# Turned copies of the first two heads' k, made behind the split of their tile

## The chip, the cores and the metric

The kernel runs on one core of one Trainium2 chip. The core has four compute engines that run beside each other, each through its own list of instructions in order: TensorE (PE: matmuls; PEld is its weight load), VectorE (DVE), ScalarE (ACT) and GpSimd (POOL). SyncE (SP) only issues transfers, and POOL and ACT issue some too. An instruction that waits holds up everything behind it in its engine's list. The metric is device time in microseconds, the median of several runs; lower is better.

## The reference, cut to what matters

A two-layer decoder trunk over 512 tokens of width 1024, all in float32. Each layer has two attention branches of 8 heads of 64, then a gated merge, an output projection and a feed-forward part (dense in layer 0, eight experts with top-2 routing in layer 1):

```python
for l in range(DEPTH):
    h = rmsnorm(x, g_mix[l]); p = h @ w_in[l]
    q_sb, k_sb, v_sb, q_fx, k_fx, v_fx, f_pre, gate_pre = jnp.split(p, splits, axis=-1)
    y_sb = merge_heads(stick_breaking_attention(q_sb, k_sb, v_sb)) @ w_o_sb[l]
    qf, kf = rmsnorm(split_heads(q_fx), g_q[l]), rmsnorm(split_heads(k_fx), g_k[l])
    y_fx = merge_heads(forgetting_attention(qf, kf, v_fx, log_f)) @ w_o_fox[l]
    x = x + (g_sb * y_sb + g_fx * y_fx) @ w_out[l]
    x = x + ffn(rmsnorm(x, g_ffn[l]))
```

In both branches a block of 128 queries meets all keys up to its end. The forgetting branch ("fox") adds a decay to each score and takes a softmax; the stick-breaking branch ("sb") turns each score into log-probabilities, sums them from the right and takes an exponential.

## The kernel before, in words

**Precision.** A float32 operand is kept as two fp32r tiles, a rounded high part and the rest, the low part. A product takes three matmuls (high by high, high by low, low by high): L320, L321, L322 in the projections.

**q and k.** The tile of two heads is split by `qk_split` into one tile for each head: the head's high part lies in its own 64 partitions, the low part in the other 64 (ACT, L524 or L526; DVE, L532 or L534). One matmul of 128 partitions then gives high by high plus low by low. The cross terms need k with its halves exchanged, the "turned" copy: `turn` makes it with two transfers of 64 partitions, issued by POOL (L542). So a score is two matmuls (L677 in fox, L768 in sb): q by k, and q by the turned k. The score of a block is complete only when the second is done.

**Fox rounds.** `fox_rounds` has 32 rounds, 8 heads by 4 query blocks, the longest block (512 keys) first. A round issues: the scores of one block into one of four PSUM tiles "pa"; the transposes (L617) of the weights from three rounds before; their split (ACT L631, DVE L633); once a head is complete, the products with v (L589, L590); the sum of score and decay with its minimum (DVE L688, tile `s` from `pa` and `cb`), the exponential (ACT L693) and the division (DVE L699, L700). The decay tile `cb` has two buffers; it is fetched by POOL (L655) and masked by POOL (L665), block by block, each mask behind the minimum of the block before.

**Weave.** PE is kept busy by a filler: between the rounds of fox stand the projections for sb's q, k and v ("mm" tiles, two of them); between the rounds of sb stand the gates and an output projection.

**What sets the order.** ACT's list stands as the program was traced. The lists of PE, DVE, POOL and SP are laid out by a scheduler at build time: it takes the instruction that its own model has ready first, and of those that are ready the one that was traced first. So where a line stands in the program decides where its instructions, and those that need their results, stand in the lists. Tiles named `b` come from one pool of 59 buffers.

**The lines in question.** `mixer` runs the fox projections (`qk_tiles`, with `qk_norm` behind each tile), then weaves `fox_rounds`, and later `sb_rounds`. In both, the turned copy of head 0 is traced when the rounds begin and that of head h+1 in the first round of head h:

```python
self.turned = {}
self.turn(k, 0)
...
if u % NT == 0:
    self.turn(k, h + 1)
```

Of the kernel before, what the change touches and what calls it, by code (L numbers as in the profile page):

```python
# [26 lines left out]
H = 8  # L27
# [45 lines left out]
def f32v(t):  # L73
    return t.bitcast(F32)


class Trunk:
# [434 lines left out]
    def qk_dst(self, a, lst):  # L512

        t = [self.blk() for _ in range(2)]
        lst.append(t)
        return t

    def qk_split(self, src, sc, *dst):
        nc = self.nc
        for h in range(2):  # L520
            s, o = slice(h * DH, h * DH + DH), slice(DH - h * DH, P - h * DH)
            t = dst[h]
            if sc == 1.0:
                nc.scalar.copy(t[s], src[s])  # L524
            else:
                nc.scalar.activation(t[s], src[s], AF.Copy, scale=sc)  # L526
        for h in range(2):
            s, o = slice(h * DH, h * DH + DH), slice(DH - h * DH, P - h * DH)
            t = dst[h]
            lo = t[o]  # L530
            if sc == 1.0:
                nc.vector.tensor_sub(lo, src[s], f32v(t)[s])  # L532
            else:
                nc.vector.scalar_tensor_tensor(lo, src[s], sc, f32v(t)[s], op0=ALU.mult, op1=ALU.subtract)  # L534

    def turn(self, k, h):

        if h < H:
            t = k[h // 2][h % 2]
            r = self.blk()  # L540
            for s, o in ((slice(0, DH), slice(DH, P)), (slice(DH, P), slice(0, DH))):
                self.nc.gpsimd.dma_start(f32v(r)[o], f32v(t)[s])  # L542
            self.turned[h] = r

    def qk_of(self, q, k, h):

        qs = q[h // 2][h % 2]
        return (qs, k[h // 2][h % 2]), (qs, self.turned[h])

    def vproj(self, hh, hl, v, rc=None, pre=None):  # L550

# [94 lines left out]
    def fox_rounds(self, q, k, v, cum, ys):  # L646
        nc = self.nc
        N = H * NT
        st = {}
        cbs = {}  # L650

        def bc(h):
            if h < H:
                cbs[h] = self.ap.tile([P, S], F32, tag="cb", bufs=2, name=self.nm("cb"))
                nc.gpsimd.dma_start(cbs[h], cum[h:h + 1].to_broadcast([P, S]))  # L655
                if CM:
                    mask(h, NT - 1)

        def idx(u):
            h, r = divmod(u, NT)  # L660
            return h, NT - 1 - r if CM else r

        def mask(h, qb):
            c = cbs[h][:, qb * P:qb * P + P]
            nc.gpsimd.affine_select(out=c, in_=c, pattern=[[-1, P]], compare_op=ALU.is_ge, fill=-NEG, base=0,  # L665
                                    channel_multiplier=1)

        def scores(u):
            h, qb = idx(u)
            if u % NT == 0:  # L670
                bc(h + 1)
                self.turn(k, h + 1)
            L = (qb + 1) * P
            qs = slice(qb * P, L)
            z = self.psa()
            for j, (a, b) in enumerate(self.qk_of(q, k, h)):
                nc.tensor.matmul(z[:, :L], a[:, qs], b[:, :L], start=j == 0, stop=bool(CM) and j == 1)  # L677
            if not CM:
                nc.tensor.matmul(z[:, qs], self.identb, self.fxmask, start=False, stop=True)
            st[u] = [z]  # L680

        def softmax_a(u):
            h, qb = idx(u)
            L = (qb + 1) * P
            z = st[u][0]
            s = self.ap.tile([P, S], F32, tag="s", bufs=NS, name=self.nm("s"))
            mn = self.sp.tile([P, 1], F32, tag="mn", name=self.nm("mn"))
            nc.vector.tensor_tensor_reduce(s[:, :L], z[:, :L], cbs[h][:, :L], 1.0, 1e38, op0=ALU.add,  # L688
                                           op1=ALU.min, accum_out=mn)
            if qb and CM:  # L690
                mask(h, qb - 1)
            sm = self.sp.tile([P, 1], F32, tag="sm", name=self.nm("sm"))
            nc.scalar.activation(s[:, :L], s[:, :L], AF.Exp, bias=mn, scale=-1.0, accum_out=sm)  # L693
            st[u] = [s, sm]

        def softmax_b(u):
            L = (idx(u)[1] + 1) * P
            s, sm = st[u]
            nc.vector.reciprocal(sm, sm)  # L699
            nc.vector.tensor_scalar_mul(s[:, :L], s[:, :L], sm)  # L700

        transposes, p_evac, av = self.attn_back(v, st, idx)
        self.turned = {}
        self.turn(k, 0)
        bc(0)
        yy = {}
        for r in range(N + FD + 3):
            if r < N:
                scores(r)
            if OB_ == 0 and r < N:  # L710
                softmax_a(r)
            if 0 <= r - SM < N and SM:
                softmax_b(r - SM)
            if OB_ == 1 and r < N:
                softmax_a(r)
            u = r - FD
            if 0 <= u < N:
                transposes(u)
            u -= 2
            if u % NT == NT - 1 and 0 <= u < N:  # L720
                yy[u // NT] = av(u // NT)
            u += 2
            if 0 <= u < N:
                p_evac(u)
            if OB_ == 2 and r < N:
                softmax_a(r)
            if r < N and not SM:
                softmax_b(r)
            u -= 3
            if u >= 0 and u % NT == NT - 1:  # L730
                self.y_evac(u // NT, yy.pop(u // NT), ys)
            yield
# [13 lines left out]
    def sb_rounds(self, q, k, v, ys):  # L746
        nc = self.nc
        N = H * NT
        st = {}
        yy = {}  # L750

        def idx(u):
            return divmod(u, NT)

        transposes, p_evac, av = self.attn_back(v, st, idx)

        self.turned = {}
        self.turn(k, 0)

        def scores(u):  # L760
            h, qb = idx(u)
            if u % NT == 0:
                self.turn(k, h + 1)
            L = (qb + 1) * P
            qs = slice(qb * P, L)
            z = self.psa()
            for j, (a, b) in enumerate(self.qk_of(q, k, h)):
                nc.tensor.matmul(z[:, :L], a[:, qs], b[:, :L], start=j == 0, stop=False)  # L768
            nc.tensor.matmul(z[:, qs], self.identb, self.sbmask, start=False, stop=True)
            st[u] = z  # L770

        def softplus(u):
            L = (idx(u)[1] + 1) * P
            z = st[u]
            a = self.ap.tile([P, S], F32, tag="sa", bufs=2, name=self.nm("sa"))[:, :L]
            nc.scalar.activation(a, z[:, :L], AF.Abs)
            nc.scalar.activation(a, a, AF.Exp, scale=-1.0)
            nc.scalar.activation(a, a, AF.Ln, bias=self.one)
            st[u] = z, a

        def logs(u):

            L = (idx(u)[1] + 1) * P
            z, a = st[u]
            s = self.ap.tile([P, S], F32, tag="s", bufs=NS, name=self.nm("s"))
            nc.vector.scalar_tensor_tensor(s[:, :L], z[:, :L], 0.0, a, op0=ALU.max, op1=ALU.add)
            nc.vector.tensor_tensor_scan(s[:, :L][:, ::-1], self.ones[:, :L], s[:, :L][:, ::-1], 0.0, op0=ALU.mult,
                                         op1=ALU.add)
            nc.vector.tensor_sub(s[:, :L], z[:, :L], s[:, :L])
            st[u] = [s]  # L790

        def weights(u):
            L = (idx(u)[1] + 1) * P
            s = st[u][0]
            nc.scalar.activation(s[:, :L], s[:, :L], AF.Exp)

        for r in range(N + SD + 3):
            if r < N:
                scores(r)
            u = r - SD  # L800
            if 0 <= u < N:
                transposes(u)
            u -= 2
            if u % NT == NT - 1 and 0 <= u < N:
                yy[u // NT] = av(u // NT)
            u += 2
            if r < N:
                softplus(r)
            if 0 <= r - SW < N and SW:
                weights(r - SW)  # L810
            if 0 <= u < N:
                p_evac(u)
            if r < N:
                logs(r)
            if r < N and not SW:
                weights(r)
            u -= 3
            if u >= 0 and u % NT == NT - 1:
                self.y_evac(u // NT, yy.pop(u // NT), ys)
            yield  # L820
# [1064 lines left out]
```

## Time and profile before

| | |
|---|---|
| median of 3 runs | 1715.91 us (1715.15 to 1716.56) |
| the profiled execution: its time, its span | 1717.1 us, 1715.3 us |
| busy share of the span: PE, PEld, DVE, ACT, POOL | 96%, 84%, 64%, 57%, 12% |
| mean granted clock of PE | 0.985 |
| scores of fox (L677), layer 0 and layer 1 (us from the span's start) | 95 to about 187, 862 to 952 |
| scores of sb (L768), layer 0 and layer 1 | 205 to about 325, 970 to 1090 |
| expert stage | from about 1205 |

The profile numbers are of one execution. The busy share is an average over stages with different limits, so what a change in one stage is worth is read in a window of that stage. In a timeline row the time in brackets is how long the engine was idle before the row, and the name behind the arrow is what ended that idle time.

### The profile page before, as it was taken

The page shows a single profiled execution, that of the slowest core. Times are in us where ns is not written, and L with a number is a line of the kernel's source. Part 1 is how long each engine was busy: PE and PEld are TensorE (multiplying, and loading weights), DVE is VectorE, ACT ScalarE, POOL GpSimd, SP SyncE. Part 2 cuts the span into 40 slices and gives each one's busy share as a digit, 9 for nine tenths or more (in the row PEclk, how much of TensorE's full clock was granted, in tenths as well). Part 3 has the DMA queues.
Part 4 walks back from the last instruction along what each step waited for, and adds up shares of the span by engine and source line. Part 5 has one row for each costly group of instructions (what it writes and reads, how often), then busy time and mean ns, then how long its engine had stood idle before and what let it go on. Part 6 is the DMA issues. An engine that isn't in the chain of part 4 may idle for free. (4 is left out here: it accounts for less than half of the span.)

```text
span 1715.3 us, 26180 instructions
## 1 busy us (share of the span) xinstructions
PE 1644.6 (96%) x9031; PEld 1433.5 (84%) x9031; DVE 1094.1 (64%) x1844; ACT 978.3 (57%) x1750; POOL 206.4 (12%) x315
## 2 busy tenths in 40 slices
PE   6989999999999999999989999999899999999996
PEld 6867987788888888888868987887789999999996
DVE  5578678765533332336578678655667888767984
ACT  5666589754422222324667589643656776656773
POOL 6112100002000000000122000101012202102200
PEclk9999999999999999999999999999799999999998
DMA  6333333235333332443433333352959999869993
GB/s 179 108 86 101 80 98 80 76 103 177 99 99 96 95 94 91 134 130 99 111 83 103 93 86 80 102 186 100 309 190 302 299 363 353 300 211 342 313 345 87
DMA packets 270840, 273.73 MB, mean 160 GB/s; under 512 B 11424, under 2 KB 259232, under 8 KB 270688
## 3 DMA queue, kind: packets, MB, share of 16 engines
q1 hardware_dynamic: 255936, 230.98, 42.7%
q0 software_dynamic: 12288, 37.40, 8.0%
q10 hardware_dynamic: 2464, 3.41, 0.6%
q8 instruction: 85, 1.39, 0.3%
q14 instruction: 67, 0.55, 0.1%
HBM read 250.21 MB, written 13.14 MB: 154 GB/s over the span
## 5 line engine op out<-in xcount | busy, mean ns | idle before, releaser
L320 PE MATMUL mm<-b,whi 128*128 128x512 f32 x1072 | 426.4, 398 | 4.1 <-DVE b L534 3.3
L322 PE MATMUL mm<-b,wlo 128*128 128x512 f32 x1072 | 419.5, 391 | 0.0
L321 PE MATMUL mm<-b,whi 128*128 128x512 f32 x1072 | 419.1, 391 | 0.0
L297 DVE TENSOR_TENSOR wlo<-wr,whi 128x1024 fp32r<-128x1024 f32 (+1 forms) x176 | 213.1, 1213 | 208.3 <-ACT whi L296 206.3
L296 ACT CAST whi<-wr 128x1024 fp32r<-128x1024 f32 (+1 forms) x176 | 182.9, 1042 | 262.9 <-issue 120.5
L1469 DVE TENSOR_TENSOR elo<-er,ehi 128x1408 fp32r<-128x1408 f32 (+3 forms) x200 | 305.1, 1568 | 26.0 <-ACT ehi L1468 15.5
L1468 ACT CAST ehi<-er 128x1408 fp32r<-128x1408 f32 (+3 forms) x200 | 256.1, 1324 | 22.3 <-DVE oh L1274 5.5
L320 PEld LDWEIGHTS mm<-b,whi 128*128 128x128 f32 x1072 | 201.8, 188 | 45.2 <-DVE b L534 4.6
L322 PEld LDWEIGHTS mm<-b,wlo 128*128 128x128 f32 x1072 | 201.3, 188 | 42.6 <-DVE wlo L297 0.4
L321 PEld LDWEIGHTS mm<-b,whi 128*128 128x128 f32 x1072 | 201.8, 188 | 39.1 <-issue 0.2
L356 PE MATMUL mm<-whi,b 128*128 128x256 f32 x320 | 92.3, 289 | 1.7 <-DVE b L532 1.1
L357 PE MATMUL mm<-wlo,b 128*128 128x256 f32 x320 | 91.3, 285 | 0.4 <-DVE wlo L297 0.4
L358 PE MATMUL mm<-whi,b 128*128 128x256 f32 x320 | 91.0, 285 | 0.0
L1682 PE MATMUL pa<-elo,ah 128*128 128x352 f32 (+1 forms) x264 | 85.8, 325 | 2.7 <-PEq L1621 0.3
L1683 PE MATMUL pa<-ehi,al 128*128 128x352 f32 (+1 forms) x264 | 84.7, 321 | 3.3 <-DVE al L1582 3.3
L1681 PE MATMUL pa<-ehi,ah 128*128 128x352 f32 (+1 forms) x264 | 86.5, 328 | 0.9 <-PEq L1689 0.2
L1647 PE MATMUL pa<-ehi,xh 128*128 128x352 f32 x256 | 85.8, 335 | 0.0
L1648 PE MATMUL pa<-elo,xh 128*128 128x352 f32 x256 | 83.7, 327 | 2.0 <-PEq L1621 0.5
L1648 PE MATMUL pa<-ehi,xl 128*128 128x352 f32 x256 | 83.1, 325 | 0.9 <-PEq L1621 0.3
L1647 PE MATMUL pa<-elo,xh 128*128 128x352 f32 x256 | 83.1, 325 | 0.3 <-DVE elo L1469 0.3
L1647 PE MATMUL pa<-ehi,xl 128*128 128x352 f32 x256 | 83.2, 325 | 0.0
L1648 PE MATMUL pa<-ehi,xh 128*128 128x352 f32 x256 | 83.1, 325 | 0.0
(351 smaller groups left out, 3107.6 us busy)
## 6 DMA issues: line engine op xcount, KB each, us to landing
er<-in_w_gu_exp_dram SPq DMA_DIRECT2D x248, 352.0 KB, 6.5
wr<-in_w_in_dram SPq DMA_DIRECT2D x80, 512.0 KB, 3.9
wr<-in_w_gu_dense_dram SPq DMA_DIRECT2D x44, 512.0 KB, 3.8
er<-in_w_dn_exp_dram SPq DMA_DIRECT2D x32, 704.0 KB, 10.6
wr<-in_w_dn_dense_dram SPq DMA_DIRECT2D x20, 512.0 KB, 3.4
er<-in_w_dn_exp_dram SPq DMA_DIRECT2D x16, 640.0 KB, 9.0
er<-in_w_dn_exp_dram SPq DMA_DIRECT2D x16, 528.0 KB, 10.2
b<-b POOLq DMA_DIRECT2D x64, 128.0 KB, 2.8
```

The source lines that it names most:

```text
L296: self.nc.scalar.copy(hi, raw)
L297: self.nc.vector.tensor_sub(lo, raw, f32v(hi))
L320: self.nc.tensor.matmul(ps, hi[:, j], hh[j], start=st, stop=False)
L321: self.nc.tensor.matmul(ps, hi[:, j], hl[j], start=False, stop=False)
L322: self.nc.tensor.matmul(ps, lo[:, j], hh[j], start=False, stop=sp)
L356: nc.tensor.matmul(o, a, hi[:, j], start=first, stop=False, skip_group_check=True)
L357: nc.tensor.matmul(o, a, lo[:, j], start=False, stop=False, skip_group_check=True)
L358: nc.tensor.matmul(o, b, hi[:, j], start=False, stop=last, skip_group_check=True)
L1468: self.nc.scalar.copy(hi, raw)
L1469: self.last_dve = self.nc.vector.tensor_sub(lo, raw, f32v(hi))
L1647: nc.tensor.matmul(pg, x[:, k], w[:, 0, kk], start=s0, stop=s1)
L1648: nc.tensor.matmul(pu, x[:, k], w[:, 1, kk], start=s0, stop=s1)
```

## The change

`qk_dst` now hands `qk_split` the list of k tiles as a third element when the tile is one of k. `qk_split` makes the turned copies of both heads of the first k tile at once, behind its own split. The copies are kept in the list of the tile itself, and `turn` skips a head that has its copy. The call at the start of the rounds is gone in both branches; heads 2 to 7 are traced where they were. The number and shape of all instructions stay the same.

```diff
         t = [self.blk() for _ in range(2)]
         lst.append(t)
-        return t
+        return t + [lst] * a
...
+        if len(dst) == 3 and dst[2][0][0] is dst[0]:
+            for h in range(2):
+                self.turn(dst[2], h)
 
     def turn(self, k, h):
 
-        if h < H:
+        if h < H and len(k[h // 2]) < 3 + h % 2:
...
-            self.turned[h] = r
+            k[h // 2].append(r)
...
-        return (qs, k[h // 2][h % 2]), (qs, self.turned[h])
+        return (qs, k[h // 2][h % 2]), (qs, k[h // 2][2 + h % 2])
...
-        self.turned = {}
-        self.turn(k, 0)
         bc(0)
```

The lists of ACT and SP keep their order. Those of PE, DVE and POOL change at the start of the fox rounds and at the start of the sb rounds, in both layers alike. Line numbers behind `qk_split` are 3 higher in the changed kernel (L677 is L680).

On PE, layer 0, this is where the scores of head 0 get their second matmul before: `b_1089` is the turned copy of head 0's k, `pa_1105` to `pa_1163` the scores of its four blocks, `mm_1243` the second tile of the filler, `s_1108` the weights of the first block.

```order
L320 MATMUL mm_1243<-b_131,whi_1010 128x512
L321 MATMUL mm_1243<-b_139,whi_1010 128x512
L677 MATMUL pa_1105<-b_1089,b_707 128x512
L677 MATMUL pa_1118<-b_1089,b_707 128x384
L677 MATMUL pa_1150<-b_1089,b_707 128x256
L677 MATMUL pa_1163<-b_1089,b_707 128x128
L322 MATMUL mm_1243<-b_131,wlo_1011 128x512
L320 MATMUL mm_1243<-b_132,whi_1010 128x512
L321 MATMUL mm_1243<-b_140,whi_1010 128x512
```

And now, 47 rows earlier in the list (`b_904` is the turned copy, `py_1065` the norm of the last but one tile of k, `mm_1137` the first tile of the filler):

```order
L502 MATMUL py_1065<-t_1043,mean_h 128x512
L680 MATMUL pa_1105<-b_802,b_707 128x512
L680 MATMUL pa_1105<-b_904,b_707 128x512
L503 MATMUL py_1065<-t_1044,mean_h 128x512
L680 MATMUL pa_1118<-b_802,b_707 128x384
L680 MATMUL pa_1118<-b_904,b_707 128x384
L320 MATMUL mm_1137<-b_126,whi_965 128x512
```

The scores of the first two blocks are complete before the filler begins, those of the other two in the middle of its first tile. The 17 matmuls of the second filler tile that are no longer ahead of the first transposes now stand between the transposes and the scores of head 1.

On DVE, layer 0, the end of the norms and splits of k and the first minima of fox, before:

```order
L507 SCALAR_TENSOR_TENSOR t_1065<-pa_963,g_k_201,t_1062 128x512
L312 TENSOR_TENSOR t_1070<-t_1067,t_1069 128x512
L532 TENSOR_TENSOR b_1006<-t_1065,b_1006 64x512
L532 TENSOR_TENSOR b_1007<-t_1065,b_1007 64x512
L507 SCALAR_TENSOR_TENSOR t_1083<-pa_1014,g_k_201,t_1080 128x512
L532 TENSOR_TENSOR b_1057<-t_1083,b_1057 64x512
L532 TENSOR_TENSOR b_1058<-t_1083,b_1058 64x512
L688 ISA s_1108,mn_1109<-pa_1105,cb_1092 128x512
```

And now:

```order
L691 ISA s_1108,mn_1109<-pa_1105,cb_1095 128x512
L691 ISA mn_1109 128x1
L507 SCALAR_TENSOR_TENSOR t_1071<-pa_969,g_k_201,t_1068 128x512
L691 ISA s_1121,mn_1122<-pa_1118,cb_1095 128x384
L691 ISA mn_1122 128x1
L312 TENSOR_TENSOR t_1076<-t_1073,t_1075 128x512
L532 TENSOR_TENSOR b_1012<-t_1071,b_1012 64x512
L532 TENSOR_TENSOR b_1013<-t_1071,b_1013 64x512
L691 ISA s_1153,mn_1154<-pa_1150,cb_1095 128x256
L691 ISA mn_1154 128x1
L507 SCALAR_TENSOR_TENSOR t_1089<-pa_1020,g_k_201,t_1086 128x512
L691 ISA s_1185,mn_1186<-pa_1163,cb_1095 128x128
```

All four minima of head 0 have moved between the norms and splits of the last two k tiles.

On POOL, layer 0, the middle of fox before, where `cb_1506` is the decay of head 4 and `b_1511` its turned copy:

```order
L542 DMA b_1511<-b_1006 64x512 x2
L655 DMA cb_1506<-cum_667 128x512
L665 AFFINE_SELECT cb_1359<-cb_1359 128x128
L665 AFFINE_SELECT cb_1506<-cb_1506 128x128
L665 AFFINE_SELECT cb_1359<-cb_1359 128x128 x2
```

And now (`b_1550` and `b_1553` are the turned copies of sb's heads 0 and 1):

```order
L545 DMA b_1511<-b_1012 64x512 x2
L658 DMA cb_1506<-cum_667 128x512
L668 AFFINE_SELECT cb_1359<-cb_1359 128x128
L545 DMA b_1550<-b_1485 64x512
L668 AFFINE_SELECT cb_1506<-cb_1506 128x128
L545 DMA b_1553<-b_1486 64x512
L545 DMA b_1550<-b_1485 64x512
L545 DMA b_1553<-b_1486 64x512
L668 AFFINE_SELECT cb_1359<-cb_1359 128x128 x2
```

The four copies of sb's first two heads stood behind the last mask of fox and now stand between the masks of heads 3 and 4. The copies of fox's heads 0 and 1 have kept their place in POOL's list, behind the first two masks.

## Rows read from the trace of the kernel before

**Rows 1.** The page: busy time, share of the span and instructions of each engine.
```profile
PE 1644.6 (96%) x9031; PEld 1433.5 (84%) x9031; DVE 1094.1 (64%) x1844; ACT 978.3 (57%) x1750; POOL 206.4 (12%) x315
```

**Rows 2.** Busy time in windows: length, engines, clock, DMA share, GB/s.
```profile
105.00:107.00 2.00, 2.00 (x12) 1.71 (x11) 0.68 (x2) 0.00 (x0) 0.00 (x0) 1.00 0.00 0
113.00:115.00 2.00, 0.80 (x3) 0.43 (x3) 0.49 (x2) 1.48 (x3) 0.32 (x2) 1.00 0.96 254
115.00:117.00 2.00, 0.78 (x3) 0.59 (x4) 1.71 (x7) 1.62 (x7) 0.64 (x3) 0.74 0.53 127
117.00:123.70 6.70, 6.61 (x24) 5.56 (x25) 6.64 (x23) 4.22 (x14) 2.17 (x3) 0.57 0.51 139
95.00:123.70 28.70, 23.62 (x101) 18.21 (x100) 21.39 (x65) 18.40 (x49) 5.61 (x12) 0.88 0.28 70
862.10:890.80 28.70, 23.87 (x106) 18.10 (x105) 21.41 (x64) 18.38 (x49) 5.59 (x12) 0.88 0.27 70
```

**Rows 3.** Timeline of PE, start of fox, layer 0: start, length, instruction, idle before.
```profile
94.68 0.57 PE L677 MATMUL pa<-b,b 128*128 128x512 f32 x2
105.78 0.74 PE L677 MATMUL pa<-b,b 128*128 128x512 f32 x4
112.18 0.41 PE L617 MATMUL pa<-ident,s 128*128 128x128 f32 x2 [1.69 <-DVE sm L699]
115.87 0.63 PE L677 MATMUL pa<-b,b 128*128 128x128 f32 x2 [2.00 <-DVE mn L688]
130.92 0.50 PE L320 MATMUL mm<-b,whi 128*128 128x512 f32 x1 [0.65 <-DVE b L534]
```

**Rows 4.** Timeline of POOL, fox, layer 0.
```profile
77.31 0.55 POOL L542 DMA_DIRECT2D b<-b  x1 [15.89 <-ACT b L524]
78.95 1.03 POOL L542 DMA_DIRECT2D b<-b  x2 [0.19 <-issue]
110.04 0.56 POOL L655 DMA_DIRECT2D cb<-cum  x1 [0.72 <-DVE mn L688]
114.69 0.53 POOL L665 TENSOR_SCALAR_AFFINE_SELECT cb<-cb 128x128 f32<-128x128 f32 x2 [3.04 <-DMA cb<-cum]
136.13 0.45 POOL L665 TENSOR_SCALAR_AFFINE_SELECT cb<-cb 128x128 f32<-128x128 f32 x1 [2.42 <-DMA cb<-cum]
139.24 0.29 POOL L665 TENSOR_SCALAR_AFFINE_SELECT cb<-cb 128x128 f32<-128x128 f32 x1 [2.66 <-DVE mn L688]
```

**Rows 5.** Timeline of DVE, layer 0; the last row is layer 1.
```profile
102.34 1.40 DVE L532 TENSOR_TENSOR b<-t,b 64x512 fp32r<-64x512 f32 x2 [0.69 <-ACT b L524]
106.32 0.69 DVE L688 CUSTOM_DVE_ANT_0 s<-pa,cb 128x512 f32<-128x512 f32 x1 [2.58 <-issue]
107.41 0.56 DVE L688 CUSTOM_DVE_ANT_0 s<-pa,cb 128x384 f32<-128x384 f32 x1 [0.40 <-POOL cb L665]
115.25 0.56 DVE L688 CUSTOM_DVE_ANT_0 s<-pa,cb 128x384 f32<-128x384 f32 x1 [1.76 <-POOL cb L665]
119.47 1.39 DVE L534 SCALAR_TENSOR_TENSOR b<-mm,b 64x512 fp32r<-64x512 f32 x2
136.74 1.39 DVE L532 TENSOR_TENSOR b<-mm,b 64x512 fp32r<-64x512 f32 x2 [0.31 <-ACT b L524]
882.38 0.56 DVE L688 CUSTOM_DVE_ANT_0 s<-pa,cb 128x384 f32<-128x384 f32 x1 [1.72 <-POOL cb L665]
```

**Rows 6.** Timeline of ACT, layer 0.
```profile
101.68 1.26 ACT L524 CAST b<-t 64x512 fp32r<-64x512 f32 x2 [0.82 <-DVE t L507]
107.05 0.72 ACT L693 ACTIVATE s<-s,mn 128x512 f32<-128x512 f32 x1 [4.10 <-DVE mn L688]
```

**Rows 7.** Windows at the start of sb, layer 0, columns as in rows 2.
```profile
200.00:220.00 20.00, 20.00 (x114) 17.28 (x113) 9.07 (x17) 9.40 (x21) 0.90 (x2) 1.00 0.40 104
```

**Rows 8.** The line of the turned copies: count, issue times, time to landing.
```profile
L542 POOL DMA_DIRECT2D b<-b x64: 522/524/545, 77.3 to 1051.4; - x64
DMA to landing us min/median/max: 2.2/2.8/6.4
```

More of the change, by code (lines that the diff above doesn't have):

```diff
@@ L755, in sb_rounds @@
         transposes, p_evac, av = self.attn_back(v, st, idx)
-        self.turned = {}
-        self.turn(k, 0)
         def scores(u):
```

## The prediction

> **What bounds the kernel now.** I read the page's busy times first: PE is busy 96% of the span [rows 1], so a gain must come out of the 70 us in which it stands, or out of stretches at half clock. Next came windows along the first attention rounds, since the change touches only their beginning. The reader should see that PE stands in one place: from 95.0 to 123.7 in layer 0 it is busy 23.62 of 28.70 us, so it idles 5.08, and in the same stretch of layer 1 it idles 28.70 - 23.87 = 4.83 [rows 2]. At 113 to 117 it works about 40% of the time, and the granted clock then falls to a mean of 0.57, near the lower level of 1.2 GHz, for 117.0 to 123.7 [rows 2]. Third, the timelines say why. PE multiplies head 0 by k at 94.68 but by the turned k only at 105.78 [rows 3], because filler stands between in its list. DVE ends the last split of k at 103.74, idles 2.58 us and takes the first minimum at 106.32 [rows 5]. ACT, idle for 4.10 us, takes the first exponential at 107.05 [rows 6]. The copies were not late: POOL issues the first at 77.31, as soon as ACT has split the tile, the last two from 78.95 on [rows 4], and the longest landing of all 64 is 6.4 us [rows 8], so they are there by 86.4. What waits is only the order of the lists.
>
> At the start of sb nothing waits: PE is busy 20.00 of 20 us from 200 to 220 at full clock [rows 7].
>
> **The change, part by part.** No instruction is added or removed. I follow layer 0.
>
> *The copies of fox's heads 0 and 1* keep their place on POOL and their time: 0.
>
> *The start of the rounds (A).* The four turned matmuls of head 0 stand right behind the first ones, at about 95 instead of 105.78. The minima are then free of PE, and DVE takes them between the norms of the last two k tiles. They fit there: from 95.0 to 123.7 DVE is busy 21.39 of 28.70 us, 7.31 idle [rows 2], and part of that lies before 103.74. The first exponential now hangs on ACT's own list: it stands behind the last split of k, which ends at 101.68 + 1.26 = 102.94 [rows 6]. The minima ahead of it (0.69 and 0.56, [rows 5]) push a low part that PE needs for the last norm; most of it goes into DVE's idle time, and I estimate a slip of 0.25. The exponential comes at 103.2 instead of 107.05: 3.85 us. Bounds: with no slip 4.1; if both minima are passed on in full (1.25), 2.85.
>
> *The decay of head 2 (B).* POOL fetches it into head 0's buffer, at 110.04, when head 0's last minimum is done. It then waits 3.04 us for the landing until 114.69, and behind that wait stands a mask of head 1 that DVE needs: DVE stands 1.76 us until 115.25 [rows 4, 5]; in layer 1 1.72 [rows 5]. Head 0's last minimum now stands before the last split of k, at about 102.3. The fetch goes out at 102.4, and with the same 4.65 us (110.04 to 114.69) the mask of head 2 runs at 107.1. The mask of head 1 is wanted only behind head 1's first minimum, near 109.6. What stays is the plain turnaround from a minimum to its mask, 0.40 [rows 5]. Gain 1.36; bounds 0 (the fetch is held up) and 1.76.
>
> *What the other engines take back (C).* ACT's list is as it was, and it has few gaps between the first exponential and the split of the filler's tile; DVE has 0.06 idle from 117.0 to 123.7 [rows 2]. I take off 0.4 for a low part that waits for ACT. So DVE's split of the filler's tile, at 119.47 [rows 5], comes 3.85 + 1.36 - 0.4 = 4.8 us earlier.
>
> *PE.* It has 17 filler matmuls left to put into the waits, and gains more than 4.8 us at first. But its next filler tile needs the PSUM that DVE splits, and at 130.92 it already waited 0.65 us for such a split [rows 3]; what it has ahead of DVE it loses there. The two stops of PE at 112.18 and 115.87 (1.69 and 2.00, [rows 3]) go with A and B. So the layer gains what DVE gains.
>
> The clock is not a term of its own. While it was low DVE was busy 6.64 of 6.70 us [rows 2], so a faster PE would have waited for DVE. The Trainium skill, "TensorE: Matmul & The Clock Gate", section "Terms", counts the penalty of a throttled stretch as its time by the share of pulses left out. By that rule the sum would be that of the second rival below; the row of DVE speaks against adding it.
>
> *The four copies of sb* now stand between masks of fox. POOL's list there waits for the split of sb's k tile, whose DVE part ends at 136.74 + 1.39 = 138.13 [rows 5]. The last copy takes 0.52 [rows 8] and is out near 138.7. The mask that stood at 136.13 slips by about 0.6, but it is of head 4, which is wanted a head later; the next is asked for at 139.24 [rows 4]: 0. The rounds and the filler move together, so this margin of 0.5 us stays.
>
> The Trainium skill, "SBUF — State Buffer", section "SBUF: two separate sides", speaks against this move: it says that POOL cannot write a transfer's descriptors while a DVE instruction holds the port that they share. The rows show no such hold: 64 copies, most of them amid DVE's work, took 522 to 545 ns to issue [rows 8].
>
> *The start of sb.* Its first score is complete 14 filler matmuls earlier, but PE has no gap there [rows 7]: 0, as long as PE stays full.
>
> Sum: 4.8 us in layer 0. Layer 1 shows the same stretch (DVE busy 21.41 of 28.70, PE idle 4.83, the same stop of 1.72): 4.8. Together 9.6. The profiled execution took 1717.1 us around a span of 1715.3; 1707.5 would be left. That execution lies 1.2 above the median of the runs, 1715.9, so I predict 1706.3.
>
> Bounds of this case: DVE's own work allows at most 7.3 us a layer (its idle time), 14.6 in all, 1701.3. Below, A at 2.85 with B at 0 and C gives 2.45 a layer, 4.9 in all, 1711.0.
>
> **The rivals.**
> 1. *Nothing comes of it.* The copies had landed 19 us before their use, so their move changes no arrival, and the earlier rounds then meet a PE that has no time left. For it: PE is full right after the stretch, and the sb half brings nothing. Against it: 7.3 us of idle DVE beside 5.1 of idle PE in one stretch [rows 2] is no bound by either. Time 1715.9.
> 2. *PE takes back all.* If PE and not DVE sets the end of the stretch, idle and half clock both return. The clock's share is 6.7 x (1 - 0.57) = 2.9 [rows 2], taken alike in both layers: 5.08 + 2.9 in layer 0, 4.83 + 2.9 in layer 1, 15.7 in all: 1700.2. Against it: DVE has no gap from 117.0 to 123.7.
> 3. *Slower: POOL stands at sb's copies.* The place is the mask asked for at 139.24, behind four copies that wait for the split of sb's k. From a lag of 0.5 us of that split behind the rounds, every us goes to the mask, the minimum and the round. With a lag of one filler tile, (136.74 - 119.47)/2 = 8.6 us [rows 5], the layer loses 8.1, against a gain of 4.8: 3.3 a layer, 6.6 in all, 1722.5. The sign turns at a lag of 5.3. For it: the rounds start earlier while the split's place in time hangs on PE. Against it: from there on the lists of PE and ACT are the same as before.
> 4. *DVE holds up POOL's issue.* If each of sb's four copies waited out a DVE instruction of 1.39 us [rows 5], 5.6 a layer would be lost, less the 0.5 of margin: 5.1 against 4.8, +0.6 in all, 1716.5. The rule that says so is the skill's, named above; 64 issues of 522 to 545 ns [rows 8] are against it.
>
> **How the numbers follow.** A measurement of this kernel can tell some 0.2% (3.4 us) from no change. Forecast (4.9 to 14.6 gained) 0.73; rival 1, 0.12; rival 2, 0.07; rival 3, 0.05; rival 4, 0.03. Faster is the forecast and rival 2, 0.80; the same rivals 1 and 4, 0.15; slower rival 3, 0.05. The forecast's own range is 1701.3 to 1711.0. With rival 2 below and a gain that is partly lost on the way to rival 1 above, I give 1700 to 1713.
>
> **What would show it.** A: the turned matmul of head 0 near 95, the first minimum near 96.5, the first exponential near 103. B: the fetch of head 2's decay near 102.4, and no stop above 0.5 us before DVE's second minimum of head 1. C: DVE's first split of the filler near 114.7. PE should idle about 3 us rather than 5 in the stretch. sb's copies should be issued near 131 to 134, with DVE waiting no longer than before for the mask behind them. Wrong it would be if the first exponential stays near 107, if a new wait of PE of over 2 us appears ahead of the first transposes, or if the gain seen at the filler's split is gone by the end of the fox rounds.

## The result, and the profile after

The changed kernel takes 1703.23 us (median of 4 runs, 1699.52 to 1704.17) against 1716.01 for the kernel before: a ratio of 0.9922 (0.9905 to 0.9939), 12.8 us. Forecast were 1706.3 and a gain of 9.6. Single executions of one program differ by 3 to 5 us, so small gains below are read inside the traces. The profiled execution of the changed kernel was the 1699.52 one, with a span of 1697.7. Up to the first copy its trace runs 0.58 us ahead of the other (POOL issues it at 76.73 instead of 77.31 [rows 4]); gains below are less these 0.58 where the text says net.

PE, layer 0, the head of the fox scores (start, length, instruction):

```profile
93.76 0.50 PE L502 MATMUL py<-t,mean_h 128*128 128x512 f32 x1
94.10 0.63 PE L680 MATMUL pa<-b,b 128*128 128x512 f32 x2
94.56 0.42 PE L503 MATMUL py<-t,mean_h 128*128 128x512 f32 x1
94.82 0.51 PE L680 MATMUL pa<-b,b 128*128 128x384 f32 x2
```

Both matmuls of a score now run as one row: the turned one is at 94, not at 105.78 [rows 3].

DVE and ACT in the same place:

```profile
95.90 0.69 DVE L691 CUSTOM_DVE_ANT_0 s<-pa,cb 128x512 f32<-128x512 f32 x1
100.99 0.28 DVE L691 CUSTOM_DVE_ANT_0 s<-pa,cb 128x128 f32<-128x128 f32 x1
108.98 0.56 DVE L691 CUSTOM_DVE_ANT_0 s<-pa,cb 128x384 f32<-128x384 f32 x1 [0.40 <-POOL cb L668]
113.19 1.40 DVE L534 SCALAR_TENSOR_TENSOR b<-mm,b 64x512 fp32r<-64x512 f32 x2
118.96 0.56 DVE L691 CUSTOM_DVE_ANT_0 s<-pa,cb 128x384 f32<-128x384 f32 x1 [0.87 <-POOL cb L668]
```

```profile
101.11 1.26 ACT L524 CAST b<-t 64x512 fp32r<-64x512 f32 x2 [0.82 <-DVE t L507]
102.39 0.72 ACT L696 ACTIVATE s<-s,mn 128x512 f32<-128x512 f32 x1
```

Head 0's four minima lie before the last split of k. The exponential follows ACT's last split without a gap, at 102.39 instead of 107.05 [rows 6]; the stop of 1.76 [rows 5] is 0.40; DVE's first split of the filler tile is at 113.19 instead of 119.47 [rows 5].

POOL, where head 2's decay is fetched, and later at sb's copies:

```profile
101.57 0.56 POOL L658 DMA_DIRECT2D cb<-cum  x1 [0.97 <-DVE mn L691]
105.12 1.04 POOL L668 TENSOR_SCALAR_AFFINE_SELECT cb<-cb 128x128 f32<-128x128 f32 x1 [2.98 <-DMA cb<-cum]
108.66 0.29 POOL L668 TENSOR_SCALAR_AFFINE_SELECT cb<-cb 128x128 f32<-128x128 f32 x1 [1.50 <-DVE mn L691]
...
129.07 0.53 POOL L545 DMA_DIRECT2D b<-b  x1 [2.67 <-ACT b L524]
129.60 0.31 POOL L668 TENSOR_SCALAR_AFFINE_SELECT cb<-cb 128x128 f32<-128x128 f32 x1
129.84 1.09 POOL L545 DMA_DIRECT2D b<-b  x2
131.12 0.52 POOL L545 DMA_DIRECT2D b<-b  x1 [0.19 <-issue]
131.91 0.29 POOL L668 TENSOR_SCALAR_AFFINE_SELECT cb<-cb 128x128 f32<-128x128 f32 x1 [0.27 <-DVE mn L691]
```

The landing is still awaited for 2.98 us, but nobody needs POOL then: the next mask, at 108.66, itself waits for DVE. sb's four copies are out at 131.64, before the mask behind them is asked for.

The stretch in windows (length, busy time of PE, PEld, DVE, ACT, POOL with their instructions, granted clock, share of the DMA engines, GB/s):

```profile
113.00:117.00 4.00, 3.98 (x22) 3.29 (x21) 3.94 (x11) 2.63 (x11) 1.09 (x2) 1.00 0.82 222
117.00:123.70 6.70, 5.69 (x30) 4.28 (x28) 5.57 (x19) 5.04 (x16) 2.75 (x7) 1.00 0.35 98
95.00:123.70 28.70, 26.68 (x132) 20.80 (x131) 25.85 (x79) 22.56 (x64) 9.52 (x19) 1.00 0.35 93
```

From 95.0 to 123.7 PE idles 2.02 us instead of 5.08 (with 132 matmuls in the window instead of 101), and the granted clock is 1.00 throughout, where it had been 0.57 for the last 6.70 us [rows 2]. PE's longest new wait there is 0.84 us, for a split of ACT; the stops of 1.69 and 2.00 [rows 3] are gone.

### The profile page after: what moved, and what is told of

The parts are those of the page before. It is cut to its first block, busy times and chain, and to the rows that moved or that the text cites. A ratio compares the mean times of both kernels' runs of the same rounds, so it can differ in the third digit from the quotient of the medians.

```text
span 1697.7 us, 26160 instructions
## 1 busy us (share of the span) xinstructions
PE 1634.0 (96%) x9031; PEld 1425.7 (84%) x9031; DVE 1093.7 (64%) x1844; ACT 977.9 (58%) x1750; POOL 205.5 (12%) x315
## 5 line engine op out<-in xcount | busy, mean ns | idle before, releaser
L1468 DVE TENSOR_TENSOR elo<-er,ehi 128x1408 fp32r<-128x1408 f32 (+3 forms) x200 | 305.1, 1569 | 26.0 <-ACT ehi L1467 15.9
```

The lines of the kernel that those rows point to most:

```text
L1468: self.last_dve = self.nc.vector.tensor_sub(lo, raw, f32v(hi))
```

## The experiments

**How a gain is read from a trace.** ACT's list is the same in all kernels here. I take the time from POOL's first copy to the start of ACT's last copy of an sb output (L598, L601 in the changed kernel), which is the end of layer 1's attention. The kernel before gives 1108.61 - 77.31 = 1031.30; a second trace of it gives 1108.67 - 77.38 = 1031.29. Column 3 is the gain by this interval, column 4 the granted clock from 110 to 125 in layer 0 and from 875 to 890 in layer 1 (in every trace here the half clock of these stages, 1.2 GHz, lies inside these two windows), columns 5 and 6 the median and the ratio to the kernel before, with its interval.

| kernel | interval | gain | clock | median us | ratio |
|---|---|---|---|---|---|
| before | 1031.30 | 0 | 0.77, 0.77 | 1716.01 | 1 |
| before, again | 1031.29 | 0.0 | 0.66, 0.77 | 1715.03 | 0.9998 (0.9989 to 1.0006) |
| sb half alone | 1031.28 | 0.0 | 0.77, 0.77 | 1715.39 | 0.9999 (0.9990 to 1.0008) |
| three decay buffers | 1032.44 | -1.1 | 0.77, 0.77 | 1716.2 | 1.0002 (0.9992 to 1.0011) |
| mask behind (B alone) | 1029.90 | 1.4 | 0.77, 0.66 | 1711.91 | 0.9977 (0.9967 to 0.9987) |
| B alone, again | 1029.15 | 2.2 | 0.77, 0.77 | 1711.77 | 0.9980 (0.9972 to 0.9989) |
| third tile (A alone) | 1027.95 | 3.4 | 0.77, 0.77 | 1709.77 | 0.9965 (0.9952 to 0.9979) |
| A alone, again | 1026.84 | 4.5 | 0.77, 0.77 | 1709.22 | 0.9971 (0.9961 to 0.9982) |
| third tile and mask behind | 1020.91 | 10.4 | 1.00, 1.00 | 1706.16 | 0.9947 (0.9935 to 0.9960) |
| head 0 alone | 1018.74 | 12.6 | 1.00, 1.00 | 1705.0 | 0.9936 (0.9923 to 0.9949) |
| fox half alone | 1018.67 | 12.6 | 1.00, 1.00 | 1703.68 | 0.9924 (0.9910 to 0.9937) |
| changed | 1018.35 | 13.0 | 1.00, 1.00 | 1703.23 | 0.9922 (0.9905 to 0.9939) |
| changed, again | 1019.29 | 12.0 | 1.00, 1.00 | 1703.57 | 0.9931 (0.9919 to 0.9944) |
| changed and mask behind | 1017.33 | 14.0 | 1.00, 1.00 | 1701.27 | 0.9911 (0.9899 to 0.9924) |

**1. The halves apart.** The fox half: the tile's list is not handed to sb's split, and sb's first copy is traced when its rounds begin.

```diff
-            self.qk_split(ps, 1.0 if a else 0.125, *dst)
+            self.qk_split(ps, 1.0 if a else 0.125, *dst[:2])
...
         transposes, p_evac, av = self.attn_back(v, st, idx)
+        self.turn(k, 0)
```

> Only the fox half of the change: the copies of fox's heads 0 and 1 are made behind their split, those of sb when its rounds begin, as before. Theory (order of PE's list at the start of fox): the whole gain is here, 12.9 us, so about 1703; first exponential of layer 0 at about 102.4, DVE's first split of the filler tile at about 113.2, as in the changed kernel. Rival (a part comes from sb's first score, which is complete 14 filler matmuls earlier): at least 2 us less gained, 1705 or more.

The sb half is the same edit on the fox side.

```diff
-        self.qk_split(qn, 1.0, *dst)
+        self.qk_split(qn, 1.0, *dst[:2])
...
+        self.turn(k, 0)
         bc(0)
```

> Only the sb half of the change; fox as before. Theory: no gain, 1716 within 1 us, since PE has no gap at the start of sb; fox's stretch from 95 to 123.7 as before (first exponential at 107.05, stop of 1.76). Rival (sb's first score counts): faster by 2 us or more. Rival (POOL stands at sb's copies): slower by 2 us or more.

Measured: 1703.68 for the fox half, all of the gain; 1715.39 for the sb half, nothing. The interval of the sb half repeats that of the kernel before to 0.02 us. Both rivals on sb are gone.

**2. Head 0 alone.**

```diff
-            for h in range(2):
+            for h in range(1):
                 self.turn(dst[2], h)
```

> The change for head 0 alone, in fox and in sb; head 1's copy is made in the first round, as before. In PE's list head 0's matmuls stand as in the changed kernel, one matmul of head 1 stands five filler matmuls later. Theory: only head 0's place counts; 1703 to 1704, first exponential at about 102.4. Rival (head 1's copy carries a part): 1705 or more.

Measured: 1705.0, which is what the rival said. But the interval, 12.6, is that of the whole change: up to the end of layer 1's attention head 0's place is what counts. What is missing is lost at the start of the expert stage (the last paragraph of the next section has the numbers); whether head 1's place has a part in that is not shown.

**3. A without B.** The copies are made behind the third tile of k. DVE's list stays as before; PE's turned matmuls stand 15 rows earlier instead of 47.

```diff
-        if len(dst) == 3 and dst[2][0][0] is dst[0]:
+        if len(dst) == 3 and len(dst[2]) > 2 and dst[2][2][0] is dst[0]:
```

> The copies of heads 0 and 1 are made behind the split of the third tile of k instead of the first. In PE's list the four turned matmuls then stand 15 filler matmuls earlier than before, not 47; DVE's list at the start of fox stays as before. Theory: term A without term B. The first minimum comes right behind the last split of k (103.74 instead of 106.32), the first exponential 2.6 earlier, but the fetch of head 2's decay still stands behind head 0's last minimum and all shifts together, so DVE's stop of 1.7 stays; DVE's first split of the filler is 2.6 earlier (116.9), 5.2 in all, about 1711. Rival (the gain hangs on the copies being made early): none of it is left, 1716. Rival (the gain is PE's clock): with the stops left the half clock stays and with it the time, 1716.

> The copies behind the third tile of k once more. The medians gave 5.7 us for A alone and 3.9 for B alone, 9.7 for both; the traces at the end of layer 1's attention gave 3.4, 1.4 and 10.4. Theory (the half clock goes only with both: with one alone PE is full at half clock in the stretch and gives part of it away): again 3 to 4 us at the end of layer 1's attention, granted clock near 0.7 from 117.0 to 123.7; the median 1710 to 1712. Rival (A and B simply add up, and the first trace was low by chance): 5 to 6 us there.

DVE of the first run:

```profile
104.32 0.69 DVE L691 CUSTOM_DVE_ANT_0 s<-pa,cb 128x512 f32<-128x512 f32 x1
113.52 0.56 DVE L691 CUSTOM_DVE_ANT_0 s<-pa,cb 128x384 f32<-128x384 f32 x1 [2.02 <-POOL cb L668]
117.73 1.39 DVE L534 SCALAR_TENSOR_TENSOR b<-mm,b 64x512 fp32r<-64x512 f32 x2
```

As expected, the idle time before the first minimum is gone and the stop stays, at 2.02. This trace runs 0.55 us behind that of the kernel before, so the filler's split is 119.47 + 0.55 - 117.73 = 2.3 us earlier. The interval gains 3.4 and 4.5, the median 5.7 and 6.1; for the second trace 3 to 4 and a time of 1710 to 1712 were expected, and 4.5 and 1709.22 came, short of the 5 to 6 of the rival. Since the copies are made about where they were made before (POOL issues them at 77.86), the gain does not come from making them early, but from PE's list.

**4. B without A.** The first attempt was a third decay buffer on the kernel before.

```diff
-                cbs[h] = self.ap.tile([P, S], F32, tag="cb", bufs=2, name=self.nm("cb"))
+                cbs[h] = self.ap.tile([P, S], F32, tag="cb", bufs=3, name=self.nm("cb"))
```

> The kernel before with three decay buffers instead of two; the lists of PE, DVE and ACT are the same, POOL fetches the decay of head 2 at the start. Theory: term B without term A. First exponential at 107.05 as before; DVE's stop of 1.76 shrinks to about 0.40; DVE's first split of the filler 1.36 earlier (118.1), 2.7 in all, about 1713. Rival (the stop is only a place where DVE waits for something else, PE or ACT): the stop comes back behind the mask, 1716.

Measured: 1716.2, no gain. It did not test B. With three buffers it is head 3's decay that waits for head 0's buffer, and it stands at the same place of POOL's list:

```profile
110.44 0.56 POOL L655 DMA_DIRECT2D cb<-cum  x1 [0.71 <-DVE mn L688]
111.00 1.04 POOL L542 DMA_DIRECT2D b<-b  x2
115.13 0.54 POOL L665 TENSOR_SCALAR_AFFINE_SELECT cb<-cb 128x128 f32<-128x128 f32 x2 [3.09 <-DMA cb<-cum]
```

The first of the two masks at 115.13 waits for the landing, the second is the one that DVE needs; DVE's stop was 1.81. What holds DVE is the order of the two masks, not the number of buffers. The second attempt changes that order alone: the mask of the next head is held behind the last mask of this one.

```diff
                 nc.gpsimd.dma_start(cbs[h], cum[h:h + 1].to_broadcast([P, S]))
-                if CM:
+                if CM and h == 0:
                     mask(h, NT - 1)
...
-                mask(h, qb - 1)
+                m = mask(h, qb - 1)
+                if qb == 1 and h + 1 < H:
+                    with self.tc.issue_after(m.ins):
+                        mask(h + 1, NT - 1)
```

> The kernel before, with the first mask of head h+1 traced, and held, behind the last mask of head h; the lists of PE, DVE, ACT and SP are the same, only POOL's differs, so that no mask that DVE is about to need stands behind the landing of a decay. Theory: term B without term A. The first exponential stays at 107.05, DVE's stop of 1.76 (1.72 in layer 1) shrinks to 0.40, DVE's first split of the filler comes 1.36 earlier (118.1), 2.7 in all, 1712.7; up to 1711 if the smaller stops of 0.89, 1.22, 0.74 and 0.59 of later heads count too. Rival (what B gives back is taken by PE or ACT behind it, as in the run with three decay buffers): no gain, 1715.5.

> The mask held behind, without the change, once more. Theory (as for the run with the third tile): 1 to 2 us at the end of layer 1's attention, granted clock near 0.7 from 117.0 to 123.7, the median 1712 to 1714. Rival (A and B add up): 3.5 to 4 us there.

```profile
106.88 0.69 DVE L688 CUSTOM_DVE_ANT_0 s<-pa,cb 128x512 f32<-128x512 f32 x1 [2.61 <-issue]
114.44 0.56 DVE L688 CUSTOM_DVE_ANT_0 s<-pa,cb 128x384 f32<-128x384 f32 x1 [0.40 <-POOL cb L665]
118.66 1.39 DVE L534 SCALAR_TENSOR_TENSOR b<-mm,b 64x512 fp32r<-64x512 f32 x2
```

The stop is 0.40, and the filler's split comes 119.47 + 0.53 - 118.66 = 1.34 us earlier, the 1.36 of term B (this trace runs 0.53 behind). The interval, however, gains only 1.4 and 2.2 over both layers together, and the medians 3.9 and 3.5. The second run again lies a little outside what was expected of it (1 to 2, and 1712 to 1714 against 1711.77).

**5. A and B together, without the change's own place.** The edit of experiment 3 and the second one of experiment 4.

> The copies made behind the third tile of k (the run above: 1709.8) and the mask of head h+1 held behind the last mask of head h. Theory: A of 2.6 and B add up: the stops of 2.02 and 1.88 become 0.40, 3.1 more than with the third tile alone, 1706.7; with the smaller later stops 1705. Rival (A and B are one wait that is counted twice): 1709.8. Rival (the order at the third tile is worth all once B is gone, since the half clock goes with the last stop): 1703.

Measured: 1706.16, as expected from the sum of the medians (5.7 + 3.9 = 9.6 against 9.7). The intervals say something else: 10.4, where the parts give 3.4 to 4.5 and 1.4 to 2.2, at most 6.7. Windows of A alone, B alone (the first trace of each) and both, layer 0:

```profile
113.00:117.00 4.00, 2.44 (x8) 1.78 (x9) 3.45 (x12) 3.33 (x12) 1.99 (x4) 0.65 0.41 95
117.00:123.70 6.70, 6.70 (x26) 5.80 (x26) 5.75 (x20) 3.34 (x12) 2.21 (x5) 0.70 0.70 182
```

```profile
113.00:117.00 4.00, 2.74 (x12) 1.73 (x10) 3.57 (x12) 2.92 (x9) 1.53 (x3) 0.64 0.88 208
117.00:123.70 6.70, 6.70 (x26) 5.19 (x26) 6.49 (x24) 4.19 (x15) 2.19 (x6) 0.71 0.68 173
```

```profile
113.00:117.00 4.00, 3.49 (x19) 2.56 (x19) 3.97 (x12) 3.96 (x15) 2.79 (x5) 1.00 0.60 151
117.00:123.70 6.70, 6.70 (x34) 5.53 (x34) 6.20 (x23) 4.15 (x13) 0.86 (x3) 1.00 0.62 167
```

With A or B alone PE still stands in the first window, the clock falls, and in the second window PE is busy for the whole 6.70 us at 0.70 and 0.71 and shows 26 matmuls; with both the clock stays at 1.00 and PE shows 34 in the same time. The second trace of B alone is an exception: there DVE is the fuller one from 117.0 to 123.7 (6.64 us against PE's 6.27), at a clock of 0.50. In every trace of the table the clock is below 1.00 in both layers where one of the two stops is left (A's, before the first minimum, or B's, before the mask), and 1.00 where neither is.

PE's own account of the interval shows where the pair wins. The rows are before, A alone, B alone, both, and the changed kernel; each holds the same 5033 matmuls.

```profile
77.31:1108.61 1031.30, 1012.20 (x5033) 839.33 (x5032) 626.36 (x1250) 579.65 (x1230) 83.86 (x171) 0.99 0.35 99
77.86:1105.81 1027.95, 1012.18 (x5033) 840.65 (x5032) 626.77 (x1250) 579.83 (x1230) 83.91 (x171) 0.99 0.36 100
77.84:1107.74 1029.90, 1013.79 (x5033) 840.39 (x5032) 626.68 (x1250) 578.98 (x1229) 84.00 (x172) 0.99 0.35 99
77.40:1098.31 1020.91, 1008.35 (x5033) 835.82 (x5032) 625.99 (x1250) 578.92 (x1230) 84.75 (x172) 1.00 0.35 100
76.73:1095.08 1018.35, 1006.49 (x5033) 835.93 (x5032) 625.93 (x1250) 579.16 (x1230) 86.01 (x171) 1.00 0.36 100
```

PE's idle time, the length less the busy time, is 19.10, 15.77, 16.11, 12.56 and 11.86. The parts take 3.3 and 3.0 off it and the pair 6.5: idle time adds up. PE's busy time does not: A alone leaves it as it was, B alone adds 1.6, and the pair takes off 3.9. (The second traces of the parts say the same: 4.3 and 2.9 off the idle time, the busy time 0.1 less and 0.7 more.) So what the pair has beyond its parts is PE's busy time for the same matmuls, and it comes in the traces without half clock. That the clock is the reason fits every trace, but no run changed the clock by itself: that step is argued, not shown.

**6. The change with the mask held behind** (the second edit of experiment 4 on the changed kernel).

> The changed kernel with the mask of head h+1 held behind the last mask of head h. In the changed kernel DVE still stands 0.87, 0.55 (layer 0) and 0.60, 0.79 (layer 1) for masks; at 0.40 each 1.2 is left to gain. Theory: B is already in the changed kernel, so at most 1.2 faster than its 1703.2: 1702 to 1703.2. Rival (a mask now waits at the turn of heads): slower than 1703.2 by 1 us or more.

Measured: 1701.27, a little less than expected. All stops of DVE for a mask are 0.40, and the interval is 14.0 instead of 12.0 and 13.0. That is the fastest version here; by the times alone (0.9899 to 0.9924) it is not apart from the changed kernel.

**7. The kernels before and changed once more.**

> The kernel before once more, for a second trace. Up to the first filler split it should repeat the first trace within 0.1 us; over all fox rounds of a layer within 1 us, as the sb half alone did, whose fox lists are the same; by the expert stage the time should differ by up to 3 us, as the traces so far do. Rival (one trace is good to 0.3 us everywhere): no such difference.

> The changed kernel once more. Theory: 12.5 to 13.5 us gained at the end of layer 1's attention, as in its first trace, granted clock 1.00 from 117.0 to 123.7; the further 3.5 us that its first trace shows in the expert stage are not of the change, so that a half-clock stretch stands near 1270 to 1290 this time and the time is 1702 to 1704. Rival (the expert stage starts better because of the change): full clock there again, 1700.

Windows from 1270 to 1280 and 1280 to 1290, at the start of the expert stage, of the changed kernel in its first trace:

```profile
1270.00:1280.00 10.00, 9.99 (x65) 9.70 (x63) 7.34 (x10) 6.03 (x8) 0.00 (x0) 1.00 0.90 293
1280.00:1290.00 10.00, 9.71 (x62) 9.50 (x63) 8.46 (x7) 5.73 (x5) 2.72 (x1) 1.00 0.87 266
```

and in its second:

```profile
1270.00:1280.00 10.00, 9.42 (x43) 8.96 (x42) 7.62 (x7) 6.40 (x8) 0.00 (x0) 0.61 0.57 173
1280.00:1290.00 10.00, 9.85 (x64) 9.59 (x64) 5.98 (x9) 3.61 (x5) 2.72 (x1) 1.00 0.58 199
```

In the second trace the half clock stands there, the span is 1703.3 and the median 1703.57. So the 1699.52 of the first profile is not of the change. In the interval the kernel before repeats to 0.01 us, the changed one only to 0.9: its second trace gains 12.0, below the 12.5 to 13.5 that were expected.

## Why the prediction was right, and where it was not

- **Copies of heads 0 and 1: 0.** Right. They are issued at the same place, and experiment 3 gains without making them earlier than before.
- **A: 3.85.** Net 107.05 - 0.58 - 102.39 = 4.08, the bound without a slip: the low parts that the minima push fell into idle time of DVE. The estimate of 0.25 for the slip was not needed.
- **B: 1.36.** Exact here (1.76 to 0.40) and by itself in experiment 4 (1.34 at the filler's split). That the stop would come back as another wait (the rival in experiment 4) is refuted up to this point.
- **C: -0.4.** Wrong, in sign. DVE's split of the filler came 119.47 - 0.58 - 113.19 = 5.7 us earlier, not 4.8; A and B give 5.44 of it, so nothing was taken back and 0.26 came on top. With A's 0.23 this is the larger part of what the forecast missed: 0.9 a layer. Layer 1 adds 5.7 and, in the second trace, 5.6 up to its first exponential of head 2.
- **PE gains what DVE gains.** Nearly. At the filler's split, where I had closed the sum, 5.7 a layer is 11.4; the interval gained 13.0 and, in the second trace, 12.0, so 0.6 to 1.6 came behind it. In which layer is not shown: the changed kernel gains 7.4 and 6.5 up to the end of layer 0's attention, but two other traces with the fox lists of before (the kernel before again, the sb half) lie 0.3 and 1.0 ahead of the first there.
- **The clock is no term of its own.** This is the step that failed. In PE's account (experiment 5) the changed kernel gains 7.24 us of idle time and 5.71 us of busy time for the same matmuls (6.27 and 5.74 in the second trace). The reason given for leaving the clock out, that DVE was busy 6.64 of 6.70 us, held for the lists of before. With one of the two stops gone PE is full there at half clock in three of four traces, and part of what DVE gains is lost. It is lost in layer 1. Up to its first exponential of head 2 (891.53 in the trace of before) A alone has gained 5.2 and 5.6 and B alone 3.8 and 3.0; by the end of the attention it is 3.4, 4.5, 1.4 and 2.2. The sb half and the three decay buffers, at half clock too, lose 0.8 and 2.1 there, the traces without half clock at most 0.5. By the working of the forecast A alone (2.6 a layer at the third tile) would have been 5.2, B alone 2.7 and the pair 7.9, where 10.4 was measured. The sum came out near because the change removes both stops, and the half clock with them; the forecast did not see that this mattered.
- **Rival 2 (PE takes back all, 15.7).** Its mechanism, idle time and clock together, was nearer than the forecast thought. Of the 9.9 us of idle time that it counted 7.2 and 6.3 went; of the 5.8 that it put on the clock PE's busy time gave 5.7. The rule of the Trainium skill that the prediction weighed, "TensorE: Matmul & The Clock Gate", section "Terms", gave this term for the clock. The measured 12.8 lies between 9.6 and 15.7, about in the middle.
- **Four copies of sb, start of sb, rivals 3 and 4: 0.** Right. The mask behind the copies waited 0.27 us for DVE, not DVE for it; the copies took 0.52 to 0.55 each; the sb half alone is worth nothing.

A alone and B alone gain about 2 us more in the median than up to the end of layer 1's attention, and head 0 alone 1.8 less (10.8 against 12.6). The traces show where: at the start of the expert stage. From ACT's last copy of an sb output to the weight split that ACT starts at 1249.62 in the trace of before (L1468), the kernel before takes 141.01 and 140.51 us, A alone 138.18 and 138.16, B alone 138.50 and 137.97, the pair 140.63, the changed kernel 140.31 and 140.40, head 0 alone 142.80. PE does 779 matmuls there in all of them. In A and B alone it is busy for 125.0 to 125.5 us instead of 127.4 and 127.7, and the granted clock from 1180 to 1230 is 0.86 in their four traces, 0.80 in the two of the kernel before and in the pair's. So the medians of A and B add up to that of the pair by coincidence: both parts have a gain of the expert stage in them that the pair has not. In head 0 alone PE is busy as before (127.80) and stands longer. Why the half clock is shorter there with one part alone, and what PE waits for with head 0 alone, stays open.

## What to carry to other kernels

When an engine stands early in a stage, read what the waiting instruction stands behind in its own list before looking at the transfer that it names: here the copies had landed 19 us early and only the order was late, and that order came from where the line was traced. Before a half-clock stretch is left out of a sum because another engine is full beside it, ask which engine will be full once that one is faster. And two stops in one stretch at half clock should be removed together before either is judged: by the end of the attention they gave 3.4 to 4.5 and 1.4 to 2.2 us one by one here, and 10.4 together.

## What the runs showed of the hardware

How long PE runs at half clock in the expert stage depends on the execution. From 1262 to 1292 the granted clock was 0.83 in the first trace of the kernel before and 0.89 in the second, 1.00 in the first trace of the changed kernel and 0.83 in its second. Single executions of the changed kernel thus differ by 3 to 5 us (1699.52 against 1702.62 to 1704.17). The 1031.3 us of the kernel before, from the first copy to the end of the attention, repeat to 0.01 meanwhile; the changed kernel's 1018.35 repeats to 0.9, and A alone to 1.1. Where a change lies early, an interval inside the trace tells more than the time of the whole, but its own spread has to be taken with a second trace.
